# Pool branch's VectorE work behind the attention stage, the last values in a bank of the scores, and value weights without a break

## The chip, the cores and the metric

The kernel runs on one core of a Trainium2 chip. TensorE (PE in the profile, its weight loads PEld) multiplies into eight PSUM banks; VectorE (DVE), ScalarE (ACT) and GpSimd (POOL) do the rest, and SyncE (SP) issues most transfers. Each engine runs its own instructions in order and waits on semaphores for the others. The metric is the device time of one execution in microseconds (us), taken as the median of several runs; the profile shows one further execution.

## What is computed

One layer of an encoder over 1024 tokens of width 1024, in float32, cut here to the part that matters:

```python
hn = rmsnorm(h, norm_mix_g[i])
z = hn @ w_in[i]
u = z[..., :POOL_W]                         # 512 columns: 4 groups of 128
q, k, v = jnp.split(z[..., POOL_W:], 3, axis=-1)   # 512 columns each: 8 heads of 64
a = pool_mixer(u, pool_w[i], pool_b[i], pool_scale[i])
o = chunk_attention(q, k, v, rel_bias[i])   # own chunk of 64 and the 8 before it
h = h + jnp.concatenate([a, o], axis=-1) @ w_out[i]
...
# gated MLP with a causal convolution, an embedding gate, a last norm
```

The pool mixer takes, per group, a trailing mean over 2, 4, 8 or 16 tokens minus the token, and multiplies by a 128x128 matrix.

## The kernel before

Every float32 product is three products of parts: each operand is split into a high part (fp32r, written by ACT) and a low part (the rest, written by DVE), and `mm3` (lines 117 to 119) adds high x high, high x low and low x high. So each weight and each activation costs ACT and DVE one pass before PE can use it (`split`, lines 122 and 123).

The attention stage is a list of units, `UNITS`: for each of the four pairs of heads first the token tiles 0 and 1 together, then the tiles 2 to 7 one by one, 28 in all. The order of PE, ACT and DVE is written out by hand in `unit(u)`. Per unit PE does this: transposes of the probabilities of the unit before (line 406), scores of this one (line 382), then some steps of the remaining input projection out of the generator `fill`, and on odd tiles the product of probabilities and values (`values`, lines 448 and 449). ACT and DVE work through lists that `push` collects with due times and `flush` writes out in the order of these times: minimum (lines 350 and 354), exponential (362), reciprocal (364), scaling (358 and 360), copies of transposed probabilities (425 and 426), evacuations of the projection (262 and 547), splits of weights for the next block (473 and 470).

`fill` runs through the projections in this order: queries and keys of pair 1, of pair 2, the values of heads 4 to 7 (`project_v`), queries and keys of pair 3, then the four pool groups 2, 3, 0 and 1 (`project_u`). A step is three products of 512 columns (six of 256 for the values). `yield True` ends a step, and `yield False` ends the unit's steps at once. The projection goes to the PSUM banks 0 and 1 in turn. Banks 2 to 7 hold transposed probabilities and scores. The products of `values` go to the one of banks 0 and 1 that the projection takes next; ACT (line 452) and DVE (line 455) empty it.

`project_u` also writes the pool branch: additions at doubling distances into the scratch tiles T1 and T2 in turn (line 560), then a scaled difference (lines 570 to 576). Groups 2 and 3 are for POOL, groups 0 and 1 for DVE; both use T1 and T2. These instructions stand in the list `later`, eight of which are written out at the end of each unit, the rest behind the last.

Behind the units PE ends the projection of group 1 (`for _ in fill`), and from there on the order of ACT and DVE is a scheduler's. Then follow the splits of the attention's output (into the places of the values), the weights of the output projection (`out_weights`, loaded at line 599 through four buffers that lie over the two buffers of `load`, line 170), the first half of the output projection and between its products `mix(g)`, which loads the pool branch's weights (`load(pool_w, 512)`), splits the pool group, multiplies and scales (line 590).

Of the kernel before, what the change touches and what calls it, by code (L numbers as in the profile page):

```python
# [73 lines left out]
NU = len(UNITS)  # L74
# [8 lines left out]
def trunk(tc, xT, pT, vecs, w_qk0, w_in, w_v, bias, counts, pool_w, w_out, w_up, w_down,  # L83
# [4 lines left out]
    with tc.tile_pool(name="sb", bufs=1) as sb, \  # L88
# [8 lines left out]
        PS = pp.tile([P, 8, 512], F32, name="PS")  # L97
# [11 lines left out]
        def f(kb, n):  # L109
            return F[:, int(kb * KW):int(kb * KW) + n]  # L110
# [46 lines left out]
        T1 = f(54.25, 272)  # L157
        T2 = f(55.3125, 272)
        otmp = f(56.375, 256)
        xraw = [f(22 + 4 * k, 1024) for k in range(KT)]  # L160
# [135 lines left out]

        later = []

        def run_later(n):
            for fn in later[:n]:  # L300
                fn()
            del later[:n]
# [128 lines left out]
        def values(u):  # L431
            nonlocal credit
            c_, ts = UNITS[u]
            w = ts[-1] // 2
            if ts[-1] % 2 == 0:
                return
            while c_ >= 2 and len(v_ready) < 2 * w + 2 or u < NU - 1 and at[0] < 1.3:
                next(fill)
                credit -= 1
                now[0] += STEP  # L440
            flush()
            ks = list(range(max(0, 2 * w - 4), 2 * w + 2))
            for j in range(2):
                pt = PT[j]
                O = PS[:, (bankn[0] + 1) % 2, 256 * j:256 * j + 256]
                for n_, k in enumerate(ks):
                    idx = k - (2 * w - 4)
                    pe.matmul(O, V[:, k, 2 * c_ + j], pt[:, 0, idx], start=n_ == 0, stop=False)  # L448
                    pe.matmul(O, V[:, k, 2 * c_ + j], pt[:, 1, idx], start=False, stop=n_ == len(ks) - 1)  # L449
            Os = [PS[:, (bankn[0] + 1) % 2, 256 * j:256 * j + 256] for j in range(2)]  # L450
            for j in range(2):
                act.activation(otmp[halves[j]], Os[j][halves[1 - j]], AF.Copy)  # L452
            for j in range(2):
                a = halves[j]
                dve.tensor_tensor(o32[a, c_, w * 256:(w + 1) * 256], Os[j][a], otmp[a], ALU.add)
# [8 lines left out]

        def split_later(ct, parts):

            t = max(5.2, now[0] + 0.4)
            for i, (src, hi, lo) in enumerate(parts):
# [6 lines left out]
        def v_weights(z):  # L475
            split_later(("v", z), [(wvr[z][:, k], wv2[z][0][:, k], wv2[z][1][:, k]) for k in (slice(0, 2), slice(2, 4))])

        def weights(ct):
# [9 lines left out]
            t = load(w_in[ct]).rearrange("p (k c) -> p k c", k=KT)  # L488
            split_later(ct, [(t[:, ks], hi[:, ks], lo[:, ks]) for ks in (slice(0, 4), slice(4, 8))])

# [23 lines left out]
        def project_v():  # L514
            v_weights(1)
            yield False
            flush()
# [26 lines left out]
        def project_u(g):  # L544
# [6 lines left out]
            win = WINDOWS[g]  # L551
            eng = pool if g >= 2 else dve
            for q in (3, 2, 1, 0):
                n = HIST + 256
                u = U[:, g, q * 256:q * 256 + n]
                src, dst, m, lo_ = u, T1, 1, 0
                while m < win:
                    lo_ += m
                    later.append(lambda d=dst[:, lo_:n], x=src[:, lo_:n], y=src[:, lo_ - m:n - m]:
                                 eng.tensor_tensor(d, x, y, ALU.add))  # L560
                    src, dst = dst, (T2 if dst is T1 else T1)
                    m *= 2
                later.append(lambda q=q, u=u, src=src: pool_out(g, q, u, src, eng))

# [123 lines left out]
        flush()  # L688
        run_later(len(later))


# [735 lines left out]
```

## Time and profile before

| | before |
|---|---|
| median of 3 runs | 1154.2 us (1153.84 to 1156.21) |
| profiled execution, its own time | 1155.19 us |
| its span | 1153.4 us |
| PE busy | 1122.8 us (97%), 5914 products |
| DVE busy | 861.3 us (75%) |
| ACT busy | 588.4 us (51%) |
| POOL busy | 144.4 us (13%) |
| mean granted clock | 0.99 |

Times of the profile run from the span's start. A row of the timeline has start, duration, engine, line, operation, written and read tile, shape, count, and in brackets how long the engine was idle before and which instruction ended that. A wait counted for a line of PE is named by the line that released it. Products are pipelined: a row of 512 columns shows 0.39 us, but the next one starts 0.23 us later.

### The profile page before, as it was taken

To read this page: it belongs to the slowest core of one execution; us is meant where nothing else is said; L and a number is where in the kernel's file an instruction comes from. 1 tells how busy PE (TensorE), PEld (TensorE's weight loads), DVE (VectorE), ACT (ScalarE), POOL (GpSimd) and SP (SyncE) were. 2 spreads that over 40 slices of the span, in tenths; PEclk is the share of its full clock that TensorE was granted. 3 is DMA by queue.
4 is the path that set the end of the run, shared out by engine and by line. 5 is a ranking of instruction groups with operands and counts; after the bars stand their busy time and mean duration, and the time that the engine had idled before them with its cause. 6 is when DMAs were issued, how large, how long until landed. Compare 5 with 4: busy or idle time off the path is not lost.

```text
span 1153.4 us, 16190 instructions
## 1 busy us (share of the span) xinstructions
PE 1122.8 (97%) x5914; PEld 939.5 (81%) x5914; DVE 861.3 (75%) x1508; ACT 588.4 (51%) x1052; POOL 144.4 (13%) x188
## 2 busy tenths in 40 slices
PE   9999898996999999999999999999999999999997
PEld 7988797885888888888888887888888888888887
DVE  8577755766846878778787878788878789986845
ACT  8376666664544555443444444444444435574634
POOL 0000000056002310021102110210021102000000
PEclk9999899998999999999999999999999999999999
DMA  7011101113520054477547755775576546620003
GB/s 278 34 37 42 38 24 37 31 38 124 185 66 28 1 165 118 144 149 174 139 144 146 173 140 144 146 173 136 151 152 164 153 138 118 177 91 19 1 24 122
DMA packets 64879, 125.91 MB, mean 109 GB/s; under 512 B 7328, under 2 KB 8736, under 8 KB 64800
## 3 DMA queue, kind: packets, MB, share of 16 engines
q1 hardware_dynamic: 50688, 99.38, 26.6%
q0 software_dynamic: 13824, 25.17, 13.9%
q8 instruction: 46, 0.75, 0.3%
q10 hardware_dynamic: 288, 0.33, 0.1%
q14 instruction: 33, 0.27, 0.1%
HBM read 110.18 MB, written 14.68 MB: 108 GB/s over the span
## 4 chain that ended last, share of the span: by engine, by line
PE 87%; DVE 5%; ACT 3%; POOL 2%; issue 2%; POOLq 0%; DVEq 0%; ACTq 0%
PE PS L117 27%; PE PS L118 27%; PE PS L119 27%; DVE R L123 1%; PE PS L448 1%; PE PS L449 1%; PE PS L382 1%; ACT B L425 1%; POOL F L560 1%; PE PS L406 1%; DVE B L426 1%; DVE F L350 1%; ACT R L122 1%; ACT F L452 0%; POOL TB L891 0%
## 5 line engine op out<-in xcount | busy, mean ns | idle before, releaser
L117 PE MATMUL PS<-R 128*128 128x512 f32 (+1 forms) x1104 | 426.5, 386 | 5.7 <-ACT R L473 2.6
L119 PE MATMUL PS<-R 128*128 128x512 f32 (+1 forms) x1104 | 422.7, 383 | 0.0
L118 PE MATMUL PS<-R 128*128 128x512 f32 (+1 forms) x1104 | 422.5, 383 | 0.0
L117 PEld LDWEIGHTS PS<-R 128*128 128x128 f32 x1104 | 208.5, 189 | 50.5 <-ACT R L473 2.8
L119 PEld LDWEIGHTS PS<-R 128*128 128x128 f32 x1104 | 208.4, 189 | 40.8 <-DVE R L470 0.4
L118 PEld LDWEIGHTS PS<-R 128*128 128x128 f32 x1104 | 208.7, 189 | 39.5 <-DVE R L227 0.2
L122 ACT ACTIVATE R<-F 128x512 fp32r<-128x512 f32 (+2 forms) x221 | 138.0, 637 | 186.0 <-PE PS L118 78.8
L123 DVE TENSOR_TENSOR R<-F,R 128x512 fp32r<-128x512 f32 (+2 forms) x221 | 152.4, 701 | 45.0 <-ACT R L122 41.8
L1126 DVE TENSOR_TENSOR F<-F,PS 128x512 f32<-128x512 f32 x140 | 92.4, 679 | 6.7 <-PE PS L119 6.5
L816 DVE TENSOR_TENSOR F<-F 128x512 f32<-128x512 f32 x88 | 60.4, 687 | 47.2 <-DMA F<-in_w_up 45.4
L122 ACT ACTIVATE BQ<-RW 128x512 fp32r<-128x512 f32 x90 | 52.6, 622 | 78.1 <-PE PS L118 74.0
L1069 POOL DMA_DIRECT2D RW<-Yd x56 | 49.7, 888 | 267.0 <-DMA RW<-Yd 205.2
L1069 POOL DMA_DIRECT2D RW<-in_w_down x40 | 36.2, 962 | 227.6 <-DMA RW<-in_w_down 191.3
L123 DVE TENSOR_TENSOR BQ<-RW,BQ 128x512 fp32r<-128x512 f32 x90 | 59.0, 683 | 2.6 <-PE PS L118 1.7
L118 PE MATMUL PS<-BQ 128*128 128x512 f32 x140 | 54.6, 390 | 0.1
L117 PE MATMUL PS<-R,BQ 128*128 128x512 f32 x140 | 54.5, 389 | 0.0
L118 PE MATMUL PS<-R,BQ 128*128 128x512 f32 x140 | 54.5, 389 | 0.0
L119 PE MATMUL PS<-BQ 128*128 128x512 f32 x140 | 54.5, 389 | 0.0
L117 PE MATMUL PS<-BQ 128*128 128x512 f32 x140 | 54.5, 389 | 0.0
L119 PE MATMUL PS<-R,BQ 128*128 128x512 f32 x140 | 54.5, 389 | 0.0
L952 ACT ACTIVATE F<-F,vec 128x1024 f32<-128x1024 f32 (+1 forms) x25 | 28.6, 1143 | 47.9 <-DVE F L927 43.3
L362 ACT ACTIVATE F<-F,small 128x640 f32<-128x640 f32 (+4 forms) x64 | 44.0, 691 | 16.8 <-DVE small L350 15.1
(179 smaller groups left out, 1707.0 us busy)
## 6 DMA issues: line engine op xcount, KB each, us to landing
F<-in_w_up SPq DMA_DIRECT2D x91, 256.0 KB, 4.0
RW<-Yd SPq DMA_DIRECT2D x60, 256.0 KB, 3.7
RW<-Yd POOLq DMA_DIRECT2D x56, 256.0 KB, 5.0
RW<-in_w_down SPq DMA_DIRECT2D x50, 256.0 KB, 2.9
RW<-in_w_down POOLq DMA_DIRECT2D x40, 256.0 KB, 6.6
Yd<-F SPq DMA_DIRECT2D x40, 256.0 KB, 3.8
F<-in_w_in SPq DMA_DIRECT2D x10, 512.0 KB, 3.5
F<-in_xT SPq DMA_DIRECT2D x16, 256.0 KB, 6.1
```

Source lines behind the costliest of these rows:

```text
L117: pe.matmul(ps, ahi, bhi, start=first, stop=False, skip_group_check=more)
L118: pe.matmul(ps, ahi, blo, start=False, stop=False, skip_group_check=more)
L119: pe.matmul(ps, alo, bhi, start=False, stop=last, skip_group_check=more)
L122: both = (act.activation(hi, src, AF.Copy), dve.tensor_tensor(lo, src, rv(hi), ALU.subtract))
L123: dve.tensor_tensor(lo, src, rv(hi), ALU.subtract))
L350: dve.tensor_tensor_reduce(S.rearrange("p (a b) -> p a b", a=2), ps, b.rearrange("p (a b) -> p a b", a=2), 1.0, BIG, ALU.add, ALU.min, s_[ ...
L362: push(1.9 + 0.85 * z, lambda S=S, s_=s_: act.activation(S, S, AF.Exp, bias=s_[:, 0:1], scale=-1.0, accum_out=s_[:, 1:2]))
L382: pe.matmul(PS[:, places[x][y], 0:wide], q[halves[x], t * P:(t + 1) * P], k[halves[x], ki + y * wide:ki + (y + 1) * wide], start=i == 0, s ...
L816: return dve.tensor_tensor(rawu[to], rawu[a], rawu[b], op)
L952: act.activation(y, Gb[:, 2 + a:2 + b], AF.Identity, bias=vec[:, C_CB + fi:C_CB + fi + 1], scale=cw(2))
L1069: pool.dma_start(t, src, accum_op=ALU.add)
L1126: dve.tensor_tensor(t, t, PS[:, 4 + d], ALU.subtract if n in (1, 5) else ALU.add)
```

## The change

Four edits, all in the attention stage. (1) The pool groups 0 and 1, DVE's, go to a list of their own, `tail`, which is written out behind the units and behind what is left of `later`; POOL's groups and DVE's have separate scratch, DVE's over a buffer of the bias that the last pairs don't use. (2) The last call of `values` writes bank 5 instead of the projection's next bank. (3) `project_v` has no `yield False` behind the splits of the second half of its weights, and these splits, as well as those of the block that follows the value projection (block 8 + 3), get the present time as their due time (`soon`) instead of 5.2 or later. (4) `values` waits for `at[0]` of 1.6 instead of 1.3, `at` being the time since the start of the present half of a projection.

```diff
--- before.py
+++ after.py
@@ -156,6 +156,7 @@
         U = f(38, 4 * (HIST + SEQ)).rearrange("p (g t) -> p g t", g=4)
         T1 = f(54.25, 272)
         T2 = f(55.3125, 272)
+        temps = [[f(57.5, 272), f(58.5625, 272)], [T1, T2]]
         otmp = f(56.375, 256)
         xraw = [f(22 + 4 * k, 1024) for k in range(KT)]
         wvraw = [f(12 + 2 * s, 512) for s in range(4)]
@@ -294,7 +295,7 @@
             return [lambda: act.activation(hi, src, AF.Copy, scale=-0.125),
                     lambda: last(lambda: dve.scalar_tensor_tensor(lo, src, -0.125, rv(hi), ALU.mult, ALU.subtract))]
 
-        later = []
+        later, tail = [], []
 
         def run_later(n):
             for fn in later[:n]:
@@ -434,20 +435,21 @@
             w = ts[-1] // 2
             if ts[-1] % 2 == 0:
                 return
-            while c_ >= 2 and len(v_ready) < 2 * w + 2 or u < NU - 1 and at[0] < 1.3:
+            while c_ >= 2 and len(v_ready) < 2 * w + 2 or u < NU - 1 and at[0] < 1.6:
                 next(fill)
                 credit -= 1
                 now[0] += STEP
             flush()
             ks = list(range(max(0, 2 * w - 4), 2 * w + 2))
+            bank = (bankn[0] + 1) % 2 if u < NU - 1 else 5
+            Os = [PS[:, bank, 256 * j:256 * j + 256] for j in range(2)]
             for j in range(2):
                 pt = PT[j]
-                O = PS[:, (bankn[0] + 1) % 2, 256 * j:256 * j + 256]
+                O = Os[j]
                 for n_, k in enumerate(ks):
                     idx = k - (2 * w - 4)
                     pe.matmul(O, V[:, k, 2 * c_ + j], pt[:, 0, idx], start=n_ == 0, stop=False)
                     pe.matmul(O, V[:, k, 2 * c_ + j], pt[:, 1, idx], start=False, stop=n_ == len(ks) - 1)
-            Os = [PS[:, (bankn[0] + 1) % 2, 256 * j:256 * j + 256] for j in range(2)]
             for j in range(2):
                 act.activation(otmp[halves[j]], Os[j][halves[1 - j]], AF.Copy)
             for j in range(2):
@@ -462,9 +464,9 @@
 
         wvr, there = [], set()
 
-        def split_later(ct, parts):
-
-            t = max(5.2, now[0] + 0.4)
+        def split_later(ct, parts, soon=False):
+
+            t = now[0] if soon else max(5.2, now[0] + 0.4)
             for i, (src, hi, lo) in enumerate(parts):
                 def low(src=src, hi=hi, lo=lo, end=i == len(parts) - 1):
                     dve.tensor_tensor(lo, src, rv(hi), ALU.subtract)
@@ -473,7 +475,8 @@
                 push(t + 0.7 * i, lambda src=src, hi=hi: act.activation(hi, src, AF.Copy), low)
 
         def v_weights(z):
-            split_later(("v", z), [(wvr[z][:, k], wv2[z][0][:, k], wv2[z][1][:, k]) for k in (slice(0, 2), slice(2, 4))])
+            split_later(("v", z), [(wvr[z][:, k], wv2[z][0][:, k], wv2[z][1][:, k])
+                                   for k in (slice(0, 2), slice(2, 4))], z == 1)
 
         def weights(ct):
 
@@ -486,7 +489,7 @@
             hi, lo = ready[ct] = wring[nw[0] % 2]
             nw[0] += 1
             t = load(w_in[ct]).rearrange("p (k c) -> p k c", k=KT)
-            split_later(ct, [(t[:, ks], hi[:, ks], lo[:, ks]) for ks in (slice(0, 4), slice(4, 8))])
+            split_later(ct, [(t[:, ks], hi[:, ks], lo[:, ks]) for ks in (slice(0, 4), slice(4, 8))], ct == 8 + 3)
 
         def project(ct, evac, wait=None):
             weights(ct)
@@ -513,7 +516,6 @@
 
         def project_v():
             v_weights(1)
-            yield False
             flush()
             for t in range(NTOK):
                 bankn[0] += 1
@@ -550,17 +552,19 @@
             yield from project(g, evac, (N_HEADS // 2 - 1, (0, 1)) if g < 2 else None)
             win = WINDOWS[g]
             eng = pool if g >= 2 else dve
+            queue = later if g >= 2 else tail
+            Ta, Tb = temps[g // 2]
             for q in (3, 2, 1, 0):
                 n = HIST + 256
                 u = U[:, g, q * 256:q * 256 + n]
-                src, dst, m, lo_ = u, T1, 1, 0
+                src, dst, m, lo_ = u, Ta, 1, 0
                 while m < win:
                     lo_ += m
-                    later.append(lambda d=dst[:, lo_:n], x=src[:, lo_:n], y=src[:, lo_ - m:n - m]:
+                    queue.append(lambda d=dst[:, lo_:n], x=src[:, lo_:n], y=src[:, lo_ - m:n - m]:
                                  eng.tensor_tensor(d, x, y, ALU.add))
-                    src, dst = dst, (T2 if dst is T1 else T1)
+                    src, dst = dst, (Tb if dst is Ta else Ta)
                     m *= 2
-                later.append(lambda q=q, u=u, src=src: pool_out(g, q, u, src, eng))
+                queue.append(lambda q=q, u=u, src=src: pool_out(g, q, u, src, eng))
 
         def pool_out(g, q, u, src, eng):
 
@@ -687,6 +691,8 @@
             flush()
         flush()
         run_later(len(later))
+        for fn in tail:
+            fn()
 
 
         for h in range(2):
```

The numbers of instructions of each engine are the same. POOL's order is the same. On PE the steps of the projection move between units. The first place is PE's rows at the start of the value projection: transposes (line 406, in the change 407), scores (382 and 383) and products of the projection (117). Before:

```order
L406 MATMUL PS<-ident,F 128x64 x20
L382 MATMUL PS<-R 128x320 x12
L406 MATMUL PS<-ident,F 128x64 x20
L382 MATMUL PS<-R 128x320 x12
L117 MATMUL PS<-R 128x256
```

In the change (behind the rows shown at L117 on PS<-R come the rest of these products, and then those of the second half of the weights):

```order
L407 MATMUL PS<-ident,F 128x64 x20
L383 MATMUL PS<-R 128x320 x12
L117 MATMUL PS<-R 128x256
L118 MATMUL PS<-R 128x256
L119 MATMUL PS<-R 128x256
```

A second pair of transposes and scores stood between the scores and the first product of the value projection; now 42 products stand there. The second place is DVE's rows at the end of the stage, with what each waits for: L547 (in the change L549) empties a bank of the projection, L470 (L472) splits weights, L560 (L564) is the pool branch's addition, L123 splits, L455 (L457) is the last values' addition. Before:

```order
L470 TENSOR_TENSOR R<-F,R 128x512 [waits DMAHW6_49,PE_49,Activation_49]
L547 TENSOR_TENSOR F<-PS,F 128x512 [waits PE_49]
L470 TENSOR_TENSOR R<-F,R 128x512 [waits Activation_49]
L560 TENSOR_TENSOR F<-F 128x271 [waits DVE_49,Pool_49]
L123 TENSOR_TENSOR R<-F,R 128x512 [waits PE_49] x4
L455 TENSOR_TENSOR F<-PS,F 64x256 [waits PE_49,Activation_49]
L455 TENSOR_TENSOR F<-PS,F 64x256
L123 TENSOR_TENSOR R<-F,R 128x512
```

In the change:

```order
L472 TENSOR_TENSOR R<-F,R 128x512 [waits DMAHW6_49,PE_49,Activation_49]
L549 TENSOR_TENSOR F<-PS,F 128x512 [waits PE_49]
L472 TENSOR_TENSOR R<-F,R 128x512 [waits Activation_49]
L564 TENSOR_TENSOR F<-F 128x271 [waits DVE_49]
L123 TENSOR_TENSOR R<-F,R 128x4x128 [waits DMAHW4_49,Activation_49]
L580 SCALAR_TENSOR_TENSOR F<-F 128x256 [waits DVE_49]
L123 TENSOR_TENSOR R<-F,R 128x512 [waits PE_49] x4
L123 TENSOR_TENSOR R<-F,R 128x512
L457 TENSOR_TENSOR F<-PS,F 64x256 [waits PE_49,Activation_49]
L457 TENSOR_TENSOR F<-PS,F 64x256
```

The pool branch's first addition no longer waits for POOL; one step of the pool branch and one split more stand ahead of the last values' addition. The third place is ACT's rows there: L473 (L475) splits weights, L122 on `B<-F 128x1024` is the copy of a pool group, L452 (L454) copies the last values. Before:

```order
L473 ACTIVATE R<-F 128x512 [waits DMAHW6_49,PE_49]
L473 ACTIVATE R<-F 128x512 [waits PE_49]
L122 ACTIVATE R<-F 128x4x128 [waits DMAHW2_49,DMAHW0_49,DVE_49]
L122 ACTIVATE R<-F 128x4x128 [waits DMAHW3_49]
L122 ACTIVATE R<-F 128x4x128 [waits DMAHW4_49]
L452 ACTIVATE F<-PS 64x256 [waits PE_49]
L452 ACTIVATE F<-PS 64x256
L122 ACTIVATE B<-F 128x1024 [waits Pool_49]
L122 ACTIVATE R<-F 128x4x128 [waits DMAHW5_49]
L122 ACTIVATE B<-F 128x1024 [waits Activation_49,Pool_49]
L122 ACTIVATE R<-F 128x512 [waits DVE_49]
```

In the change:

```order
L475 ACTIVATE R<-F 128x512 [waits DMAHW6_49,PE_49]
L475 ACTIVATE R<-F 128x512 [waits PE_49]
L122 ACTIVATE R<-F 128x4x128 [waits DMAHW4_49,DVE_49]
L122 ACTIVATE R<-F 128x4x128 [waits DMAHW7_49,DMAHW0_49,DVE_49]
L122 ACTIVATE R<-F 128x4x128 [waits DMAHW1_49]
L122 ACTIVATE B<-F 128x1024 [waits PE_49,Pool_49]
L122 ACTIVATE B<-F 128x1024 [waits PE_49,Activation_49,Pool_49]
L454 ACTIVATE F<-PS 64x256 [waits PE_49]
L454 ACTIVATE F<-PS 64x256
L122 ACTIVATE R<-F 128x4x128 [waits DMAHW5_49]
L122 ACTIVATE R<-F 128x512 [waits DVE_49]
```

The copies of the last values stood ahead of both copies of pool groups, which wait for POOL; now they stand behind them.

## The prediction

> **What bounds the kernel now.** I read the busy shares first, then what TensorE (PE) waited for, then the stretches around those waits. The shares (busy us, share of the span, instructions):
>
> ```profile
> span 1153.4 us, 16190 instructions
> PE 1122.8 (97%) x5914; PEld 939.5 (81%) x5914; DVE 861.3 (75%) x1508; ACT 588.4 (51%) x1052; POOL 144.4 (13%) x188
> ```
>
> PE sets the time: 1153.4 - 1122.8 = 30.6 us is all the idle time it has. The change adds and removes no instruction; it can only take idle and half-rate time from PE, or add some. PE's waits (total, times, longest):
>
> ```profile
> PE PS L117 <- DVE F L455: 9.4, 1, 9.4
> PE PS L406 <- DVE F L360: 5.5, 2, 4.9
> PE PS L117 <- ACT R L473: 2.6, 1, 2.6
> ...
> PE PS L117 <- ACT B L425: 1.3, 2, 0.7
> PE PS L448 <- DVE F L262: 1.1, 2, 0.6
> ```
>
> Three of them lie where the edits are: 9.4 us before the bank of the last values is free, 4.9 us (of the 5.5) at the value weights, 2.6 us at the weights behind the value projection. Next, the stretches around these three, and the rest of the kernel: length, busy time of PE, PEld, DVE, ACT and POOL, then the granted clock (PEclk, a number alone), DMA share, GB/s.
>
> ```profile
> 129.90:134.80 4.90, 0.00 (x0) 0.00 (x0) 4.36 (x11) 2.73 (x7) 0.00 (x0) 0.85 0.00 0
> 134.80:140.10 5.30, 5.28 (x43) 4.95 (x44) 3.08 (x7) 3.61 (x9) 0.00 (x0) 0.50 0.28 99
> 176.90:179.50 2.60, 0.04 (x1) 0.00 (x0) 2.09 (x8) 2.60 (x8) 0.00 (x0) 1.00 0.00 0
> 179.50:186.00 6.50, 6.44 (x41) 4.54 (x42) 2.50 (x5) 2.50 (x6) 0.00 (x0) 0.74 0.44 160
> 286.00:290.40 4.40, 4.40 (x11) 3.43 (x12) 4.40 (x10) 0.48 (x1) 0.00 (x0) 0.50 0.93 302
> 400.00:1153.00 753.00, 745.32 (x3384) 618.97 (x3383) 591.66 (x912) 348.11 (x564) 93.08 (x103) 1.00 0.51 130
> ```
>
> Behind each wait the clock falls. A stretch of length L at clock c loses L(1-c): 5.30 x 0.50 = **2.65 us** behind the first, 6.50 x 0.26 = **1.7 us** behind the second, 4.40 x 0.50 = **2.2 us** behind the third. From 400 us on PE is busy 745.32 of 753 and nothing is edited, so what PE gains before 345 us stays gained.
>
> **Term A: no break at the value weights.** The broken loop left PE nothing to do until the next unit's transposes, which need this unit's softmax (rows: start, duration, engine, line).
>
> ```profile
> 131.26 0.83 ACT L362 ACTIVATE F<-F,small 128x640 f32<-128x640 f32 x1 [0.90 <-DVE small L350]
> 132.50 1.61 DVE L426 TENSOR_TENSOR B<-PS,B 128x640 fp32r<-128x640 f32 x3
> 134.82 1.33 PE L406 MATMUL PS<-ident,F 64*128 64x64 f32 x20 [4.94 <-DVE F L360]
> ```
>
> PE's scores ended at 134.82 - 4.94 = 129.9. Now the value projection goes on there. Its first four k steps use weights split long ago: 12 products of 256 columns, which take 1.44 us (0.12 each) by these two rows, 12 products apart.
>
> ```profile
> 170.01 0.28 PE L117 MATMUL PS<-B,R 128*128 128x256 f32 x1
> 171.45 0.28 PE L117 MATMUL PS<-R 128*128 128x256 f32 x1
> ```
>
> So PE runs to 131.3 and then needs the second half of the value weights. ACT's order is now: first exponential, both splits, second exponential. The exponential ends with its sum at 132.1 and the splits, 0.57 each by their row in term B, at 132.7 and 133.2. DVE writes the low parts behind the first of the three L426 (132.50, some 0.75): 133.25 + 0.65 = 133.9; then come two more L426 and a reciprocal to 134.8, and the second low part at 135.4. PE waits 1.4 + 1.0 + 0.8 = 3.2 us in pieces instead of 4.94; the softmax for the next transposes is ready at 136.3, PE there only at 138. Gain 4.94 - 3.2 = 1.7. The clock: 3.2 us idle within 4 is like the 2.62 us at 176.9, which a loss of 1.7 followed, so 2.65 - 1.7 = 0.95. **A = 2.7**; bounds 1.7 (clock loss as before) and 4.4 (none).
>
> **Term B: weights behind the value projection split at once.** The splits were held back until after the softmax's scaling:
>
> ```profile
> 178.89 1.14 ACT L473 ACTIVATE R<-F 128x512 fp32r<-128x512 f32 x2
> ```
>
> Now they stand in the unit in which the last value tile's first half ends. Behind them come that unit's values, then transposes, scores and six products before their first use, over 2 us of PE work for splits of 0.57 each. **B = 2.62 + 1.7 = 4.3.** Without that cover, the price is that of before.
>
> **Term C: the last values get bank 5.** Call T the time at which PE could go on behind the last values (276.4 before, 0.12 behind its row) and O the start of the output projection (299.0).
>
> ```profile
> 276.30 0.28 PE L449 MATMUL PS<-B,R 128*128 128x256 f32 x1
> 281.27 0.44 DVE L560 TENSOR_TENSOR F<-F 128x271 f32<-128x271 f32 x1 [6.23 <-POOL F L560]
> 284.97 0.85 DVE L455 TENSOR_TENSOR F<-PS,F 64x256 f32<-64x256 f32 x2
> 285.97 0.76 PE L117 MATMUL PS<-R,B 128*128 128x512 f32 x1 [9.38 <-DVE F L455]
> 299.00 0.39 PE L117 MATMUL PS<-R 128*128 128x512 f32 x1
> ```
>
> DVE stood 6.23 us at L560, the pool branch's first addition, until POOL released the scratch T1; behind it in DVE's queue lay four splits and then L455, which empties the bank that PE wants. With bank 5 PE no longer asks: its scores have been read, and its next writer is an output product well behind O. The scratch is separate, too, so DVE doesn't stop there. **C = 9.38 + 2.2 = 11.6**; the 0.85 us of L455 lies beside PE's projection. O comes at T + 10.2: 45 products are left, at 0.227 us each (24 of them lie between the PE rows 299.00 above and 304.44 below).
>
> **Term D: what is late next.** DVE has some 12 us less for the same work before O. The gate is the pool branch's weights: their load goes to a buffer that DVE must first have read.
>
> ```profile
> 299.90 0.33 SPq L170 DMA_DIRECT2D F<-in_pool_w  x1
> 302.50 0.63 ACT L122 ACTIVATE B<-F 128x512 fp32r<-128x512 f32 x1 [1.78 <-DMA F<-in_pool_w]
> 304.44 0.39 PE L117 MATMUL PS<-B 128*128 128x512 f32 x1
> ```
>
> Before, this was O + 0.9 (load issued), O + 3.5 (landed), O + 5.4 (used), without a wait. Now follow POOL's last group, ACT's copies and DVE's queue:
>
> ```profile
> 264.07 3.00 POOL L560 TENSOR_TENSOR F<-F 128x271 f32<-128x271 f32 x4 [6.03 <-issue]
> 279.35 0.77 ACT L452 ACTIVATE F<-PS 64x256 f32<-64x256 f32 x2
> 283.37 1.13 POOL L574 TENSOR_TENSOR F<-F 128x240 f32<-128x240 f32 x1
> 284.54 1.06 ACT L122 ACTIVATE B<-F 128x1024 fp32r<-128x1024 f32 x1 [2.82 <-POOL F L574]
> 288.69 0.68 DVE L123 TENSOR_TENSOR R<-F,R 128x512 fp32r<-128x512 f32 x1
> 289.29 0.43 DVE L560 TENSOR_TENSOR F<-F 128x271 f32<-128x271 f32 x1
> 289.64 0.68 DVE L123 TENSOR_TENSOR R<-F,R 128x512 fp32r<-128x512 f32 x1
> 291.53 1.22 DVE L123 TENSOR_TENSOR B<-F,B 128x1024 fp32r<-128x1024 f32 x1
> ```
>
> POOL takes 283.37 + 1.13 - 264.07 = 20.4 us. It can start when its values leave PSUM, now one unit earlier, at T - 18.6: values 24 x 0.12 = 2.9, a unit of 5.2 + 0.8 (term E), transposes 0.7, 27 products 6.1, values 2.9. So it ends at T + 1.8; I take T + 2.5, as DVE is busy beside it all the time. ACT's order has changed there: its copy of the pool group (1.06) waits for POOL *ahead of* the two copies of the last values (0.77), behind which it stood before. So DVE's addition starts at T + 4.3 and ends at T + 5.2. Then, up to the read that frees the buffer, DVE has five splits and two evacuations (0.60 each, by the starts of the rows 288.69 and 289.29), six steps of the pool branch (0.35), two splits of 1024 columns (1.2) and bits: 8.8 us, to T + 14.0 = O + 3.8. The load lands 2.6 later, at O + 6.4; ACT's half is there at O + 7.0, DVE's (3.6 us of queue, then 0.6) at O + 8.0. PE wants them at O + 5.45: it waits 1.55, and 0.55 more at its third product. **D = -2.1.** Bounds: if POOL ends by T + 1, DVE never stops and the wait is 0.7; at T + 5 it is 4.6, with a clock loss of 1.7 on top. The first output products also need four output weights from this queue, the last at T + 9.3 against T + 12.7: no wait.
>
> **Term E: shorter cover in some units.** The steps shift between units (values pass at 1.6 instead of 1.3, and no unit goes without). A unit needs this long from its transposes to the next ones:
>
> ```profile
> 259.46 0.83 PE L406 MATMUL PS<-ident,F 64*128 64x64 f32 x20
> 265.56 0.91 DVE L360 TENSOR_SCALAR F<-F,small 128x640 f32<-128x640 f32 x1
> ```
>
> 7.0 us with an evacuation in DVE's way, some 6.1 without. PE's own part is 1.8 for transposes and scores plus its products. Four units now have fewer of these: pair 1, tile 7 (30 narrow ones for 42; 1.8 + 3.6 = 5.4 against 6.5: 1.1 us), pair 2, tile 2 (0.45), pair 3, tile 3 (12 wide ones for 18: 0.9) and pair 3, tile 7 (15 for 21: 5.2 against 6.1, 0.8). That is 3.3 us. Against it, 1.3 on L425 and 0.5 of those on L262 belong to the old places. **E = -1.5**, bounds -4 and +1.8.
>
> **Sum.** 2.7 + 4.3 + 11.6 - 2.1 - 1.5 = **15.0**. The profiled execution took 1155.2 in all (span 1153.4), so 1140.2; the median of the three runs shown is 1.0 below it, at 1154.2, and I forecast **1139.2 us**. All at their good ends: 4.4 + 4.3 + 11.6 - 0.7 + 1.8 = 21.4, 1132.8. All at their bad ends: 1.7 + 4.3 + 11.6 - 6.3 - 4 = 7.3, 1146.9.
>
> [...]
>
> [...]
>
> ```profile
> 229.22 1.29 DVE L470 TENSOR_TENSOR B<-F,B 128x512 fp32r<-128x512 f32 x2 [0.89 <-ACT B L473]
> 267.01 1.71 DVE L470 TENSOR_TENSOR B<-F,B 128x512 fp32r<-128x512 f32 x2 [0.53 <-ACT B L473]
> ```
>
> Each split took 0.21 us more. [...]
>
> **Rivals.**
> 1. *All of it is hidden* (20%). POOL ends early, units are long enough, no clock is lost. For it: PE ran from 299.00 to 304.44 without a wait, all of it fed in time. Against it: DVE's order puts 8.8 us ahead of the load. 1154.2 - 20 = 1134.
> 2. *DVE becomes the bound behind the stage* (16%): POOL ends at T + 5 to T + 7, D is -6 with the clock, E is -3. 15.0 - 4 - 1.5 = 9.5: 1144.7.
> 3. *The stall only moves* (4%), and the edit doesn't do what it says: the output weights come too late behind the addition in DVE's queue, and PE stands at O. Some 3 us of C are left, 6 in all: 1148.
> 4. *Slower* (2%): ACT's copy waits for POOL ahead of the last values' copy, and DVE's queue waits for that. Each us of POOL's end beyond T + 2.5 costs one; it turns the sign beyond T + 17.5, when POOL would need 36 us for its 20.4. At T + 22 the time would be 1158.7.
>
> **Chances.** Forecast 58% (1136.5 to 1142.5), then 20, 16, 4 and 2. Range **1133 to 1147**, the bounds above. A difference of 0.2% (2.3 us) is about what a measurement of this kernel tells from none: faster 0.97, same 0.01, slower 0.02.
>
> **What would show it.** A: no transposes wait near 134, but value products wait two or three times from 131.3. B: no wait on the split behind the value projection, and no fallen clock there. C: a product follows the values at T without a gap. D: the first product on pool weights waits 1 to 4 us for ACT, then DVE. E: waits of about 1 us at the transposes after short units. POOL's last addition well after T + 5, or a wait at O, would make the forecast wrong.

## The result, and the profile after

The changed kernel takes **1139.2 us** (median of 4 runs, 1138.33 to 1139.81) where the kernel before took 1154.0 us beside it (4 runs, 1153.41 to 1156.21): a ratio of 0.9868, with a 95% interval of 0.9851 to 0.9885. The forecast was 1139.2. The sum was right; the experiments below show that its largest term was put down to the wrong edit.

The head of the page of the changed kernel (its profiled execution took 1138.94 us in all):

```profile
span 1137.2 us, 16199 instructions
PE 1119.2 (98%) x5914; PEld 936.4 (82%) x5914; DVE 863.7 (76%) x1508; ACT 588.7 (52%) x1052; POOL 144.3 (13%) x188
```

PE's idle time fell from 30.6 to 1137.2 - 1119.2 = 18.0 us, and its busy time fell by 3.6 us with the same 5914 products, of which fewer ran at a fallen clock (before, 0.50 for 5.30 us, 0.74 for 6.50 and 0.50 for 4.40; now 0.89 for 4.80 us and 0.67 for 3.50). What PE waited for in the changed kernel (total, times, longest):

```profile
PE PS L407 <- DVE F L361: 2.7, 5, 0.9
...
PE PS L118 <- DVE B L472: 1.3, 2, 0.8
PE PS L117 <- ACT B L122: 1.1, 1, 1.1
PE PS L117 <- ACT B L475: 1.1, 1, 1.1
```

The waits of 9.4, 4.9 and 2.6 us are gone. In their place stand three short ones for the value weights (1.1 on L475 and 0.8 and 0.5 on L472), one of 1.1 for the pool branch's weights (L122), and more small ones at the transposes (L361). The windows of the changed kernel at those places (length, busy time of PE, PEld, DVE, ACT, POOL, then the granted clock, DMA share, GB/s):

```profile
131.70:136.50 4.80, 2.43 (x13) 1.83 (x13) 4.41 (x11) 3.36 (x7) 0.00 (x0) 0.89 0.00 0
136.50:140.00 3.50, 3.50 (x23) 3.37 (x22) 0.48 (x1) 0.50 (x2) 0.00 (x0) 0.67 0.46 150
172.00:180.00 8.00, 7.66 (x74) 6.31 (x73) 6.27 (x18) 6.96 (x16) 0.29 (x2) 1.00 0.19 66
180.00:186.00 6.00, 5.82 (x39) 4.59 (x36) 5.24 (x12) 4.75 (x10) 0.00 (x0) 1.00 0.29 87
287.00:292.00 5.00, 3.92 (x17) 2.64 (x16) 5.00 (x12) 3.42 (x6) 0.00 (x0) 1.00 0.75 235
400.00:1137.00 737.00, 729.26 (x3314) 606.37 (x3312) 580.08 (x892) 340.14 (x551) 89.16 (x101) 1.00 0.51 130
```

The clock still falls behind the value weights (4.80 x 0.11 + 3.50 x 0.33 = 1.7 us lost); in every other stretch up to 1130 us it is 1.00. From 400 us on PE idles 737.0 - 729.26 = 7.7 us, as before (753.0 - 745.32): all that was gained lies ahead of that. Rows of the changed kernel behind the stage (start, duration, engine, line):

```profile
251.28 0.68 DVE L549 TENSOR_TENSOR F<-PS,F 128x512 f32<-128x512 f32 x1
252.20 3.85 POOL L564 TENSOR_TENSOR F<-F 128x271 f32<-128x271 f32 x4
271.52 0.28 PE L452 MATMUL PS<-B,R 128*128 128x256 f32 x1
271.64 0.40 PE L117 MATMUL PS<-R,B 128*128 128x512 f32 x1
271.88 1.14 POOL L578 TENSOR_TENSOR F<-F 128x240 f32<-128x240 f32 x1
275.30 0.85 DVE L457 TENSOR_TENSOR F<-PS,F 64x256 f32<-64x256 f32 x2
281.87 0.39 PE L117 MATMUL PS<-R 128*128 128x512 f32 x1
285.09 0.33 SPq L171 DMA_DIRECT2D F<-in_pool_w  x1
288.55 0.50 PE L117 MATMUL PS<-B 128*128 128x512 f32 x1 [1.08 <-ACT B L122]
```

The product behind the last values follows them without a gap (T = 271.64), though the addition L457 that empties their bank runs only at 275.30. O is 281.87, T + 10.2 as forecast. POOL's last group started at 252.20, right behind the evacuation of its values at 251.28, and ended at T + 1.4. The pool weights' load is issued at O + 3.2 and PE waits 1.08 us for it.

### The profile page after: what moved, and what is told of

Read it like the earlier page. It is cut to its first block, busy times and chain, and to the rows that moved or that the text cites. A ratio compares the mean times of both kernels' runs of the same rounds, so it can differ in the third digit from the quotient of the medians.

```text
span 1137.2 us, 16199 instructions
## 1 busy us (share of the span) xinstructions
PE 1119.2 (98%) x5914; PEld 936.4 (82%) x5914; DVE 863.7 (76%) x1508; ACT 588.7 (52%) x1052; POOL 144.3 (13%) x188
## 4 chain that ended last, share of the span: by engine, by line
PE 88%; DVE 6%; ACT 3%; issue 2%; DMA 1%; POOL 0%; SPq 0%; POOLq 0%; DVEq 0%; ACTq 0%
PE PS L117 28%; PE PS L118 27%; PE PS L119 27%; DVE B L427 2%; DVE F L351 2%; PE PS L451 1%; PE PS L452 1%; ACT B L426 1%; PE PS L383 1%; PE PS L407 1%; ACT F L454 1%; DVE R L123 0%; PE PS L739 0%; DMA F<-in_xT 0%; ACT F L359 0%
## 5 line engine op out<-in xcount | busy, mean ns | idle before, releaser
L117 PE MATMUL PS<-R 128*128 128x512 f32 (+1 forms) x1104 | 425.6, 386 | 1.7 <-ACT F L909 0.8
L117 PEld LDWEIGHTS PS<-R 128*128 128x128 f32 x1104 | 208.2, 189 | 45.1 <-issue 2.1
L122 ACT ACTIVATE R<-F 128x512 fp32r<-128x512 f32 (+2 forms) x221 | 138.1, 638 | 175.2 <-PE PS L118 80.2
L123 DVE TENSOR_TENSOR R<-F,R 128x512 fp32r<-128x512 f32 (+2 forms) x221 | 152.8, 703 | 37.3 <-ACT R L122 35.9
L122 ACT ACTIVATE BQ<-RW 128x512 fp32r<-128x512 f32 x90 | 52.6, 622 | 77.1 <-PE PS L118 73.1
L123 DVE TENSOR_TENSOR BQ<-RW,BQ 128x512 fp32r<-128x512 f32 x90 | 59.0, 683 | 2.1 <-PE PS L118 1.3
L117 PE MATMUL PS<-BQ 128*128 128x512 f32 x140 | 54.5, 389 | 0.0
L117 PE MATMUL PS<-R,BQ 128*128 128x512 f32 x140 | 54.5, 389 | 0.0
L958 ACT ACTIVATE F<-F,vec 128x1024 f32<-128x1024 f32 (+1 forms) x25 | 28.6, 1143 | 48.6 <-DVE F L933 42.9
L363 ACT ACTIVATE F<-F,small 128x640 f32<-128x640 f32 (+4 forms) x64 | 44.0, 691 | 16.7 <-DVE small L351 15.0
```

The source lines that it names most:

```text
L117: pe.matmul(ps, ahi, bhi, start=first, stop=False, skip_group_check=more)
L122: both = (act.activation(hi, src, AF.Copy), dve.tensor_tensor(lo, src, rv(hi), ALU.subtract))
L123: dve.tensor_tensor(lo, src, rv(hi), ALU.subtract))
L363: push(1.9 + 0.85 * z, lambda S=S, s_=s_: act.activation(S, S, AF.Exp, bias=s_[:, 0:1], scale=-1.0, accum_out=s_[:, 1:2]))
L958: act.activation(y, Gb[:, 2 + a:2 + b], AF.Identity, bias=vec[:, C_CB + fi:C_CB + fi + 1], scale=cw(2))
```

## The experiments

All times are medians; each group ran beside the kernel before, and "less" is one minus the ratio to it, times 1154.2 us. T, O and the terms A to E are those of the prediction.

| kernel | us | ratio to before, 95% interval | less |
|---|---|---|---|
| the change | 1139.2 | 0.9868 (0.9851 to 0.9885) | 15.2 |
| bank 5 alone | 1151.4 | 0.9975 (0.9965 to 0.9984) | 2.9 |
| scratch and tail alone | 1150.4 | 0.9968 (0.9958 to 0.9978) | 3.7 |
| bank 5, scratch and tail | 1151.3 | 0.9979 (0.9970 to 0.9988) | 2.4 |
| weights' edits alone | 1139.9 | 0.9877 (0.9863 to 0.9891) | 14.2 |
| of these, break removed alone | 1143.1 | 0.9899 (0.9886 to 0.9913) | 11.7 |
| of these, early splits alone | 1151.9 | 0.9987 (0.9978 to 0.9995) | 1.5 |
| weights' edits, DRAIN 8 | 1141.8 | 0.9900 (0.9888 to 0.9913) | 11.5 |
| before, DRAIN 10 | 1150.2 | 0.9975 (0.9965 to 0.9985) | 2.9 |
| change, threshold 1.3 | 1139.1 | 0.9870 (0.9856 to 0.9884) | 15.0 |
| change, DRAIN 8 | 1139.0 | 0.9871 (0.9856 to 0.9885) | 14.9 |
| change, early pool weights | 1137.6 | 0.9854 (0.9841 to 0.9868) | 16.9 |
| combined | 1135.4 | 0.9832 (0.9817 to 0.9846) | 19.4 |

### Bank 5 alone

```
-            ks = list(range(max(0, 2 * w - 4), 2 * w + 2))
+            ks, bank = list(range(max(0, 2 * w - 4), 2 * w + 2)), (bankn[0] + 1) % 2 if u < NU - 1 else 5
...
-                O = PS[:, (bankn[0] + 1) % 2, 256 * j:256 * j + 256]
+                O = PS[:, bank, 256 * j:256 * j + 256]
```

The same bank stands in the line for `Os`; scratch and order are those of the kernel before.

> Only the last values' bank is changed: bank 5 in the kernel before, scratch and order as before. Theory (term C needs all its parts): the product behind the values follows at T without a gap, so the 9.4 us wait on L455 is gone, but DVE still stands some 6 us at its first pool addition until POOL releases T1 at 281.3. Some 13.8 us of DVE's work then lie ahead of the read that frees the buffer of the pool branch's weights, which is read at about 295 where O is now 286.6; the load lands at 298 and the first product on pool weights, due at O + 5.45 = 292.0, waits 6 to 8 us. Gain 11.6 less 7 less a clock loss of about 2 less 1 at O: 1 to 5 us, 1149 to 1153. Rival (the bank alone was what held PE): no wait of over 2 us appears behind the stage and the gain is 9 to 11.6, 1142.5 to 1145.

Measured 1151.4 us, 2.9 less. Rows of this kernel:

```profile
264.11 3.00 POOL L560 TENSOR_TENSOR F<-F 128x271 f32<-128x271 f32 x4 [6.02 <-issue]
276.35 0.28 PE L449 MATMUL PS<-B,R 128*128 128x256 f32 x1
276.47 0.40 PE L117 MATMUL PS<-R,B 128*128 128x512 f32 x1
281.36 0.44 DVE L560 TENSOR_TENSOR F<-F 128x271 f32<-128x271 f32 x1 [6.28 <-POOL F L560]
289.54 0.50 PE L119 MATMUL PS<-R 128*128 128x512 f32 x1 [0.83 <-DVE R L123]
291.55 0.50 PE L119 MATMUL PS<-R 128*128 128x512 f32 x1 [1.04 <-DVE R L123]
296.42 0.33 SPq L170 DMA_DIRECT2D F<-in_pool_w  x1
299.82 0.50 PE L117 MATMUL PS<-B 128*128 128x512 f32 x1 [4.08 <-ACT B L122]
```

There is no gap at T any more, and most of what was won there is given back behind O: 0.83 + 1.04 + 4.08 = 5.95 us of waits (the last was expected at 6 to 8), and 1.7 us of clock behind the last (8 us at 0.79, from 296 to 304). 11.6 - 7.7 = 3.9, which is at the edge of the measured interval. DVE still stood 6.28 us at T1, so its queue was late at everything that came next. The rival, on which term C rested, falls: the bank is what PE waited for, and it isn't what the time depended on.

### Scratch and tail alone

```
+        temps = [[f(57.5, 272), f(58.5625, 272)], [T1, T2]]
+            queue = later if g >= 2 else tail
+            Ta, Tb = temps[g // 2]
```

With the lines of the change that use them; the last values stay in the projection's bank.

> Only the scratch of its own for DVE's pool groups and their place behind the stage; the last values stay in the bank of the projection. Theory (the 9.4 us had two causes in a row, DVE's stop at T1 and the bank): DVE no longer stops at its first pool addition, but the product behind the values still waits for the addition that empties the bank, which now follows ACT's copies of the last values; these stand behind loads of the output weights in ACT's queue and end at 280.1 as before. The wait is 4 to 5 us instead of 9.4, with the same fall of the clock behind it; the gain is 3.5 to 5.5 us, 1148.5 to 1150.5. Rival (DVE's stop was all of it): the wait is under 1.5 us and the gain 9 to 11.6. Rival (the bank was all of it): the wait stays at 9 us, gain under 1.

Measured 1150.4 us, 3.7 less: as the theory had it.

```profile
281.55 0.86 DVE L457 TENSOR_TENSOR F<-PS,F 64x256 f32<-64x256 f32 x2 [1.21 <-ACT F L454]
282.55 0.77 PE L117 MATMUL PS<-R,B 128*128 128x512 f32 x1 [5.69 <-DVE F L457]
```

DVE passed its first pool addition without a stop and waited for ACT's copy of the last values instead, so PE waited 5.69 us (expected 4 to 5) and not 9.38. The profiled execution is the slowest of this kernel's ten, at 1154.5; some 2.5 us of it are waits far behind the stage (3.4 us on L910, where the other profiles show at most 1.6), so only its rows are used here.

### The weights' edits alone

```
-            t = max(5.2, now[0] + 0.4)
+            t = now[0] if soon else max(5.2, now[0] + 0.4)
...
             v_weights(1)
-            yield False
```

`soon` is true at the value weights' second half and at block 8 + 3, as in the change.

> Only the two edits at the weights: no break ahead of the value projection, and both splits (value weights, and the weights behind the value projection) pushed at once. Theory: terms A + B = 2.7 + 4.3 = 7.0 us, of which some 2.6 is clock that no longer falls; 1146 to 1148, with the waits near 133 in three pieces and none near 177, and the 9.4 us wait untouched. Rival (the clock falls as before whatever the length of the gap): 1.7 + 2.6 = 4.3, 1149 to 1150.5.

Measured **1139.9 us, 14.2 less**: twice what the theory gave (7.0) and three times what the rival gave (4.3), without bank 5, without scratch and with the old threshold. Its interval and that of the change overlap, so what the other edits add in the change can't be told from nothing. The longest of PE's waits is now this one, and the 9.4 us are gone:

```profile
PE PS L117 <- ACT B L122: 1.7, 1, 1.7
```

Rows of this kernel around T:

```profile
249.90 0.68 DVE L547 TENSOR_TENSOR F<-PS,F 128x512 f32<-128x512 f32 x1
250.81 3.21 POOL L560 TENSOR_TENSOR F<-F 128x271 f32<-128x271 f32 x4
...
270.42 0.28 PE L449 MATMUL PS<-B,R 128*128 128x256 f32 x1
270.54 0.40 PE L117 MATMUL PS<-R,B 128*128 128x512 f32 x1
273.69 0.86 DVE L455 TENSOR_TENSOR F<-PS,F 64x256 f32<-64x256 f32 x2
```

The break was itself one step of the projections: `yield False` used up a credit and issued no product. Without it every later step stands one step earlier against the units. That moves two things. First, the last values: before, they closed a half of a projection, and the next product opened the next half in the very bank that they had written. Now one step of a half (three products) stands ahead of them and 21 products of it follow, in the other bank; theirs is asked for at 270.54 + 21 x 0.23 = 275.4, and L455 has emptied it by 274.55. Second, POOL: its last group needs the evacuation of the fourth half of its values. That is now done in the unit before, at 249.90. In the kernel before it was this row:

```profile
263.25 0.69 DVE L547 TENSOR_TENSOR F<-PS,F 128x512 f32<-128x512 f32 x1
```

That is 13.35 us, of which the stage's own end moved 5.88 (T is 276.42 there and 270.54 here); the other 7.5 us are a unit. So POOL ends at 270.4 where it ended at 284.5, and DVE never stands at T1. This became the theory for the next runs: the removed break is worth a bank and a scratch.

### Bank 5, scratch and tail

The two edits above together in the kernel before, with its break, late splits and threshold.

> The kernel before with bank 5 and the scratch and place of DVE's pool groups, without the two edits at the weights and the threshold: term C with all its parts, alone. Theory formed after the first four runs (the removed break moves POOL's last group one unit earlier; without it POOL ends 8 us behind T and what PE doesn't wait for at T it waits for later): no gap at T = 276.4, O near 287.3; DVE's addition waits for ACT until 281.5, ten us of DVE's queue lie ahead of the read that frees the pool weights' buffer, so the first product on pool weights waits 4 to 5 us; 1147 to 1149.5. Rival, the prediction's term C and D as they stand there (11.6 - 2.1): 1144 to 1145.5, with a wait of 1 to 2 us at the pool weights.

Measured 1151.3 us, 2.4 less. Rows of this kernel:

```profile
275.74 0.40 PE L117 MATMUL PS<-R,B 128*128 128x512 f32 x1
284.26 0.70 POOL L579 TENSOR_TENSOR F<-F 128x240 f32<-128x240 f32 x1
290.30 0.50 PE L119 MATMUL PS<-R 128*128 128x512 f32 x1 [1.04 <-DVE R L123]
298.47 0.50 PE L117 MATMUL PS<-B 128*128 128x512 f32 x1 [3.94 <-ACT B L122]
```

Term C with all its parts, alone, is worth a quarter of the 9.5 us that the prediction had for it less D. POOL ends at T + 9.2 and the time goes at the pool weights (3.94 us and the clock behind it, 0.79 from 296 to 304), as the new theory said; the gain is smaller than it said, 1.4 to 3.5 us by the interval where 4.7 to 7.2 were expected. The profiled execution took 1149.3, two under the median of its eleven runs, so where the other executions lose that is not seen.

### Early splits alone

The weights' edits with `yield False` kept.

> The kernel before with only the early pushing of the two splits; the break stays. Theory: this is term B alone, the 2.6 us wait near 177 and the fallen clock behind it go, 4.9 and 9.4 us stay: 3.5 to 4.5 us, 1149.5 to 1151. The rest of what the weights' edits gave alone (14.4 - 4.3 = 10) is then the break's. Rival (the early pushing also moves what comes behind, and is most of the 14.4): 1140 to 1144.

Measured 1151.9 us, 1.5 less: under the range. Its waits in rows:

```profile
136.09 1.33 PE L406 MATMUL PS<-ident,F 64*128 64x64 f32 x20 [6.07 <-DVE F L360]
179.04 0.50 PE L117 MATMUL PS<-R 128*128 128x512 f32 x1 [0.95 <-ACT R L473]
283.94 0.76 PE L117 MATMUL PS<-R,B 128*128 128x512 f32 x1 [9.38 <-DVE F L455]
```

The wait near 177 fell from 2.62 to 0.95 us and the clock behind it stayed at 1.00 (176.8 to 186; 2.62 - 0.95 + 1.7 = 3.4 gained), but the splits now stand ahead of the second exponential, and the break's wait grew from 4.94 to 6.07, which takes 1.1 us of it back. That the early pushing is most of the gain is refuted: the break's removal is.

### Break removed alone

```
             v_weights(1)
-            yield False
```

> The kernel before without the break and nothing else; both splits are pushed late as before. Theory (the removed break moves the last values by one step and POOL by one unit, whatever becomes of the splits): no wait of over 1 us at T, POOL's last addition within 2 us of T; the value products wait some 4 us near 133 and the split near 177 costs 2.6 and its clock again; 1144 to 1147.5. Rival (the early pushing is needed for the gain behind the stage too): 1150 to 1154, with a wait of several us at T.

Measured **1143.1 us, 11.7 less, by one deleted line**. Its longest waits:

```profile
PE PS L117 <- ACT B L473: 4.0, 1, 4.0
PE PS L117 <- ACT B L122: 2.1, 1, 2.1
```

There is no wait at T (273.36), and POOL's last addition ended at 273.2, T - 0.2. Nor is there one near 177, which the theory had left in: one step earlier, the weights are pushed for splitting a unit sooner, ACT has them split by 175.6, and the first product on them comes at 177.94. So the break's removal is enough for all of term B, and the time came out under the 1144 expected; the early splits alone were enough for 3.4 of its 4.3. With the early splits on top (14.2) the 4.0 us become 2.4 in pieces, 2.5 us in all.

### Where the last values stand: DRAIN 8 and 10

```
-    DRAIN = 9
+    DRAIN = 8
```

The last unit issues DRAIN steps ahead of the last values. With 8 in the kernel with the weights' edits, the values close a half again while POOL stays early; with 10 in the kernel before, they stand one step into a half while POOL stays late.

> The two edits at the weights as in the third run, and one projection step fewer in the last unit (8 for 9), so that the last values stand at the end of a half again, as in the kernel before, and the next product goes into the bank that they wrote; POOL stays a unit early. Theory (the step mattered: the bank is asked for at once or 21 products later): a wait on the addition that empties the bank comes back at T, 3 to 4 us since ACT's copy ends near 273, with 1 us or more of clock behind it; 1143 to 1145. Rival (POOL a unit early is all of it): no wait of over 1 us at T, 1139.5 to 1140.5.

> The kernel before with one projection step more in the last unit (10 for 9) and nothing else: the last values stand one step into a half, as in the changed kernel, while POOL stays late. Theory (step and POOL's time each carry a part): no gap at T = 277.1, DVE stands at T1 until 281.3 as before, the bank is asked for 4.8 us behind T and free at 286.2, so PE waits 4 to 4.5 us there instead of 9.4; gain 4 to 5.5 us, 1148.5 to 1150.5. Rival (the step is all of it): no wait of over 1 us, gain 10 or more. Rival (POOL's time is all of it): the wait stays near 9, gain under 1.

Measured 1141.8 and 1150.2 us. The row of the first, and of the second:

```profile
274.51 0.47 PE L117 MATMUL PS<-R,B 128*128 128x512 f32 x1 [4.75 <-DVE F L455]
```

```profile
287.39 0.77 PE L117 MATMUL PS<-R,B 128*128 128x512 f32 x1 [4.63 <-DVE F L455]
```

Either alone leaves about half of the 9.38 us. In the first, 4.75 us at T (3 to 4 were expected) cost only 2 to 3 us in the end, as there is no wait on the pool weights behind it, where the kernel with 9 steps waited 1.70 us with the same fall of the clock (1.7 us lost in either): 4.75 - 1.70 = 3.05. So it came out under the 1143 to 1145 expected; that POOL's time is all of it is refuted. In the second the step is worth 2.9 us while POOL is late (expected 4 to 5.5).

> The changed kernel with one projection step fewer in the last unit (8 for 9): the last values stand at the end of a half, where the kernel with the weights' edits alone waited 4.8 us at T. Theory (bank 5 is worth a wait in this place and nothing in the other): no wait at T, 1138.5 to 1140.0, so 2 to 3 us under the kernel of the seventh run. Rival (bank 5 is worth nothing here either, what was given up at T was given back later): 1141 to 1142.5.

This is the change with DRAIN 8. Measured 1139.0 us: no wait at T (270.65), and 14.9 us less than before where the kernel with the weights' edits and DRAIN 8 has 11.5. The kernels also differ in scratch, tail and threshold, but it is the bank that the wait was for. In this place the edit earns something: the kernel is indifferent to where in a half the last values stand.

### The threshold, and the pool weights

```
-            while c_ >= 2 and len(v_ready) < 2 * w + 2 or u < NU - 1 and at[0] < 1.6:
+            while c_ >= 2 and len(v_ready) < 2 * w + 2 or u < NU - 1 and at[0] < 1.3:
```

> The changed kernel with the threshold of the values back at 1.3, so that five projection steps stand one unit later. Theory (term E is the price of this edit): the waits at the transposes of pair 1 tile 7 and pair 3 tile 7 (0.89, 0.72) and those of 0.3 to 0.45 go, and the waits of the first values behind an evacuation (0.5 to 0.7 each) come back; the net is 1.1 to 1.5 us faster than the changed kernel, 1137.5 to 1138.3. Rival (the edit pays for itself, the waits it takes away are worth more than those it adds): 1139.5 to 1141.

Measured 1139.1 us against 1139.2: no difference that can be told, and neither what the theory nor what the rival expected. In its profile T is 269.86, 1.8 us earlier than in the change, so term E is there in that place; but PE then waits 1.62 us instead of 1.08 for the pool weights, so part of it is given back. Where the rest goes isn't settled: each interval is 3 to 4 us wide.

```
+        pw = f(12, 512)
+        sp.dma_start(pw, pool_w)
...
-                t = load(pool_w, 512)
-                split(t, pwh, pwl)
+                with tc.high_priority(AHEAD):
+                    split(pw, pwh, pwl)
```

The load stands behind the stage, ahead of the output projection.

> The changed kernel with the pool branch's weights loaded ahead of time into a place of their own (that of the first bias, which nothing reads any more there) and split at O, ahead of the output weights that follow. Theory (term D is the late load): the waits of 1.1 and 0.4 us at the first products on pool weights go and no other takes their place, ACT's and DVE's halves being there at O + 1 and O + 3 where PE asks at O + 5.4; 1.2 to 1.8 us under the changed kernel, 1137.3 to 1138.0. Rival (something else is as late: the pooled groups or the output weights): a wait of 1 us or more on another tile at the same place, and 1138.6 to 1139.6.

Measured 1137.6 us, 1.6 under the change, as expected, though the two intervals overlap. The waits on the pool weights are gone and PE is busy through the window in which it idled 1.08 us:

```profile
287.00:292.00 5.00, 5.00 (x23) 3.97 (x23) 4.91 (x12) 2.94 (x5) 0.00 (x0) 1.00 0.77 224
```

The two profiled executions lie only 0.2 us apart (1138.74 and 1138.94). In this one PE waits longer on L909 (1.3 us for 0.8) and on a split of L123 (0.8 us for none), so the waits are shown to go, and the size of the gain in the median is not.

### A combined version

```
-                    if (h, k) == (0, 2):
+                    if (h, k) == (0, 2) and ct != 1:
                         weights(behind)
```

With the early pool weights and the threshold at 1.3. The last projection block (ct 1) has no successor, and `weights(None)` loads and splits the second half of the value weights again, which nothing reads there.

> The early pool weights of the ninth run, the threshold back at 1.3, and the second load of the value weights left out, which the last projection block issues though nothing reads it (two loads of 512 KB and two splits on ACT and DVE). Theory: the waits of the ninth run stay away, ACT's and DVE's queues ahead of T are 1.1 and 2.2 us shorter, and the output weights come sooner; 1136.5 to 1138.0, at or below the ninth run. Rival (POOL's end decides what follows, and with the order shifted ACT's copies wait for POOL ahead of more output weights): a wait of 1 us or more at O on the output weights, 1138.5 to 1140.

Measured **1135.4 us** (5 runs, 1133.54 to 1136.73), faster than both kernels and under the 1136.5 to 1138.0 expected: its interval ends at 0.9846, below that of the change. Its T is 270.36, and no wait on the output weights or the pool weights is left. Which of the two edits beyond the early pool weights brings the further 2 us wasn't tried apart, and against the kernel with these weights alone the intervals still overlap.

## Why the prediction was right, and where its reasons were not

**The total.** By the rows of the changed kernel, worked out as in the prediction, it is 3.5 + 4.3 + 11.6 - 1.6 - 1.1 = 16.7, against 1155.19 - 1138.94 = 16.25 between the two profiled executions and 14.8 between the medians. Every term was within 0.8 us of its size; that the forecast met the median to a tenth is luck. What failed is what the largest term was put down to.

**A, 2.7.** Right in mechanism, and a little small: the waits were 1.07, 0.82 and 0.48 us for the 1.4, 1.0 and 0.8 forecast, and the clock lost 1.7, so 4.94 - 2.37 + 0.95 = 3.5. What was overlooked is the larger effect of the same line, one step of shift for all that follows.

**B, 4.3.** The size is right, and the cause named is one of two that each would have done. Pushing early with the break kept left 0.95 us of the 2.62 and took the fall of the clock away (1.00 for the 0.74 of before), but made the break's wait longer; removing the break alone took the whole wait away, though the split was pushed late.

**C, 11.6.** This step failed: "With bank 5 PE no longer asks", and "The scratch is separate, too, so DVE doesn't stop there". Both are true and neither was needed. The profile named L455 and POOL's T1 as what was waited for, and the prediction took the edits that remove these two dependences to be what removes the time. But both were late only because the last values closed a half and POOL's last group had been fed a unit late, and one removed step ended that. Edited alone, C's parts moved the wait to the pool weights: 2.4 us were left of the 11.6. That is nearly the third rival, put at 4%: the stall moved, though mostly to the pool weights and not to the output weights that the rival names. The prediction even had the cause in hand: it wrote, under D, that POOL's values leave PSUM "now one unit earlier", and used it only to place POOL's end.

**D, -2.1.** Right mechanism, a little too dear: POOL ended at T + 1.4 where T + 2.5 was taken (0.7 us of it for a busy DVE, the author's estimate, which no run shows), the load went out at O + 3.2 (3.8), the first product on the pool weights came at 288.55 where its turn was 287.31, and the two behind it were 0.38 us late in all: 1.6. With the load out of that queue these waits were gone.

**E, -1.5.** By the rows -1.1: new waits of 0.89 (1.1 forecast), 0.39 (0.9), 0.72 (0.8) and small ones, against 2.3 that went. Undone, it changed nothing that can be measured; part of what the units gained came back as a longer wait at the pool weights, and the rest is open.

**The rivals.** All hidden (1134) didn't happen; the combined version, with further edits, comes within 1.4 us of it. DVE as the bound behind the stage didn't: five of its splits, the first two beside POOL, took 0.71 us each, and POOL, for which this rival took T + 5 to T + 7, ended at T + 1.4; no run shows what would have brought T + 7. Of the prediction's two pairs of splits the second (1.71 us at 267.01) ran beside POOL, whose rows go on from 264.07, and the first (1.29 us at 229.22) didn't, as POOL stood idle from 216.5 to 241.7: 0.21 us for each split.

## What to carry to other kernels

Where one generator feeds fillers into the units of another, a step that does nothing is a shift of everything behind it: before a stall far down the program is put down to the buffer named in the trace, count where in its bank's turn, and in which unit, each side would stand after the edit. A wait removed at one place is worth what the queue behind it can follow; undo each edit alone, and test an edit in the kernel without the others before it gets the credit. A load that has to wait for a shared buffer at the start of a stage can be given a place of its own, as here, where the waits behind it went.

## What the runs showed of the clock

The clock didn't fall in proportion to a gap. Behind the 1.70 us wait of the kernel with the weights' edits (ended 288.07) these windows of 1 us follow:

```profile
288.00:289.00 1.00, 0.78 (x3) 0.34 (x3) 1.00 (x3) 0.03 (x2) 0.00 (x0) 1.00 0.87 252
289.00:290.00 1.00, 1.00 (x3) 0.80 (x4) 0.93 (x3) 0.92 (x2) 0.00 (x0) 0.59 0.67 188
290.00:291.00 1.00, 1.00 (x4) 0.80 (x3) 1.00 (x3) 1.00 (x3) 0.00 (x0) 0.50 0.95 313
291.00:292.00 1.00, 1.00 (x4) 0.71 (x3) 0.99 (x3) 1.00 (x3) 0.00 (x0) 0.50 0.67 168
292.00:293.00 1.00, 1.00 (x5) 0.81 (x4) 0.77 (x2) 1.00 (x3) 0.00 (x0) 0.71 0.74 252
```

It lost 0.41 + 0.50 + 0.50 + 0.29 = 1.7 us. The same 1.7 us followed the gap of 4.75 us (weights' edits, DRAIN 8), that of 2.08 us (break removed alone) and that of 4.08 us (bank 5 alone). More was lost in the kernel before behind its gaps of 4.94 us (2.65) and 9.38 us (2.2).

Behind the gap of 1.62 us in the change with the threshold at 1.3 the clock stayed at 1.00, as behind those of 1.08 us (the change) and 0.95 us (early splits alone). But in the changed kernel it was 0.89 in the stretch with the three shorter ones of 1.07, 0.82 and 0.48 us (131.70 to 136.50) and 0.67 in the 3.50 us behind it. So the length of a single gap doesn't decide; what does is not shown.
